# A decoder trunk on one core: S5 parameters and tables, the rows of a shift, and a hold on POOL are moved

## The chip, the core and the metric

The kernel runs on one core of a Trainium2 chip. The metric is the device time of one execution in microseconds; smaller is better. The core has five engines that work side by side and wait for each other through semaphores: TensorE (PE: matmuls, its weight loads are listed as PEld), VectorE (DVE), ScalarE (ACT), GpSimd (POOL) and SyncE (SP, which issues most of the loads). Each engine runs its own instructions strictly in order; an instruction that waits holds up all that stand behind it on its engine.

## What is computed

A trunk of two layers over 512 tokens of width 1024, in float32. Layer 0 mixes the tokens with an S5 state space (32 groups of 16 channels, 64 complex states each) and with HGRN2 (4 heads) side by side, layer 1 with gated linear attention; each mixer is followed by a SwiGLU FFN. In front of each sub-layer stands a norm whose gain and shift come from a conditioning vector c. What matters here is the start of layer 0:

```python
cond = jax.nn.silu(c)
mod = cond @ ada_w[layer] + ada_b[layer]
shift_m, scale_m, gate_m, shift_f, scale_f, gate_f = jnp.split(mod, N_MOD, axis=-1)
h = modulate(rms_norm(x, norm_mix_g[layer]), shift_m, scale_m)
z = h @ ev_w_in[e]
u, hq, hf, hi, hg = jnp.split(z, ...)
# S5: delta = exp(log_step); lam_bar = exp(lam * delta); b_bar = ((lam_bar - 1) / lam) * b
#     states by a linear recurrence over the tokens, y = Re(c . states) + d * u
```

## The kernel before

A float32 product with a weight is made from three matmuls on fp32r halves: high part by high part, low by high, high by low (`proj`, lines 275 to 277). So h is held as `hhi` and `hlo`, and each weight is loaded raw, copied into a high part by ACT (`wsplit`, `whi`) and subtracted into a low part by DVE (`wlo`).

**The gates.** The first norm needs gain (`gsc`) and shift (`mod`) of layer 0. `ada_first` makes them in two halves of 512 columns: half 0 gives the gain and shift of the first four of h's eight tiles, half 1 those of the other four. For each half 16 tiles `ar` of 128x512 are loaded. Eight belong to the scale and are summed up on DVE into `acc` (lines 111 and 116: each instruction adds `ar` times a column of `cond`). Eight belong to the shift. In half 0 all eight are multiplied on PE, as single-row matmuls into `row` (line 405; such a float32 matmul shows as two records). In half 1 (`n` = 4) the first four go to PE and the other four to DVE, into a second sum `acs`. Then small matmuls against ones fold `acc`, `row` (copied to `rsb`) and `acs` into columns (lines 416, 419, 421), and three DVE instructions make `mod` and `gsc`.

**The first products.** x is transposed on PE (`xps`), normalized into `xn` (two blocks by DVE, two by ACT) and transposed again (`xnps`). `norm_out` makes, for each tile of h, `hhi` on ACT, `ht` and `hlo` on DVE. Four projections `u` of S5 (q = 0 to 3) follow: `u_part` does the first four of eight k of one q, the rest is done when the second half of h is there. Behind them come the projections `hq`, `hf`, `hv`, `hg` of HGRN2, head by head, and between these the four blocks of S5.

**S5.** `s5_params` makes the parameters of all groups from `prow` (lambda), `lsrow` (log step) and `drow`: transposes into `pps`, a copy `pc`, then some 70 small DVE instructions (`s5s`, `s5L`), most of 128x16. `s5_tables(q)` makes cosine and sine tables of 128x512 for block q: four products on POOL (`ph` from `s5s` and the index tile `cidx`; `ph` less its rounding; a second product into the `cos` tile; `ph` plus that), on DVE a rounding (`cos<-ph`) and a clamp (`ph<-ph`), on ACT an absolute value and two sines. `s5_in_out` and `s5_mats(q)` make the matrices of block q, mostly on POOL (`s5b`, `bv`, `B`, `W`), copied by ACT into zeroed tiles (`Bd`, `Wd`), transposed on PE (`wnp`) and copied to `wn`. `s5_block` then copies u into `U` (ACT, 16 small pieces), makes `vps` on PE from `wn` and `U`, rotates by the tables, scans on DVE, rotates back, and makes `yp` on PE and `yf` on ACT.

**What sets the order.** The kernel is written as a program; a scheduler puts each engine's instructions in an order from its own estimate of when inputs are there. The code can bend it: `with after(ins):` keeps what is issued inside behind the instruction `ins`, and `tc.high_priority(offset=-3000)` around `s5_params` makes its work yield to all other work. `hold` is a small copy on POOL: with `after(hold)` POOL's work of S5 stands behind it. In the kernel before, one hold waits for the first gate (line 938, for the matrices) and one for the second (line 1001, for the tables). Activation tables are loaded on ACT when a function of another set is next (line 101); exp belongs to one set, silu and sine to another, and `tact` keeps such calls in the order of the code.

Of the kernel before, what the change touches and what calls it, by code (L numbers as in the profile page):

```python
# [8 lines left out]
F32 = mybir.dt.float32  # L9
# [8 lines left out]
P = 128  # L18
# [23 lines left out]
def trunk(  # L42
# [90 lines left out]
    nc.sync.dma_start(out=rows1[112:128, :], in_=norm_ffn_g.rearrange("l (k p) -> (l k) p", p=P))  # L133
    nc.scalar.dma_start(out=rows2[12:16, :], in_=s5_b_glu.rearrange("o (k p) -> (o k) p", p=P))
    nc.scalar.dma_start(out=rows2[16:28, :], in_=hg_lb_logits.rearrange("o (k p) -> (o k) p", p=P))
    nc.scalar.dma_start(out=rows2[28:32, :], in_=od_b_a.rearrange("o (k p) -> (o k) p", p=P))
    nc.scalar.dma_start(out=rows2[8:12, :], in_=s5_d.rearrange("o (k p) -> (o k) p", p=P))

    prow = tt("prow", "s", (16, 4, P))
# [28 lines left out]

    tps = ps_a("tps")
    PE.transpose(tps[:, 0:32], rows2, ident[0:32, 0:32])  # L170
    V.tensor_copy(out=cols2, in_=tps[:, 0:32])
    tact(cond, cols2[:, 0:8], AF.Silu)
    tps = ps_a("tps")
    PE.transpose(tps[:, 0:P], rows1, ident)
    V.tensor_copy(out=cols1, in_=tps[:, 0:P])

# [212 lines left out]

    def ada_first(half, ws, rows=(), n=KT):  # L390


        acc = tt(f"acc01{half}", "sc")
        acs = tt(f"acc00{half}", "X") if n < KT else None
        fp = ps_a(f"row{half}")
        row = fp[0:1, :]
        last = None
        for k in range(KT):
            c_ = cond[:, k : k + 1]
            if k == 0:  # L400
                tsv(V, acc, ws[0], c_, ALU.mult)
            else:
                stt(acc, ws[2 * k], c_, acc, ALU.mult, ALU.add)
            if k < n:
                ins = PE.matmul(row, lhsT=c_, rhs=ws[2 * k + 1], start=(k == 0), stop=(k == n - 1))
            elif k == n:
                tsv(V, acs, ws[2 * k + 1], c_, ALU.mult)
            else:
                stt(acs, ws[2 * k + 1], c_, acs, ALU.mult, ALU.add)
            if k + 1 in rows:  # L410
                last = rows[k + 1](ins)
        rsb = tt(f"rsb{half}", "sc")[0:1, :]
        act(rsb, row, AF.Copy)
        with after(last):
            for m in range(4):
                PE.matmul(fp[:, m : m + 1], lhsT=acc[:, m * P : (m + 1) * P], rhs=ones[:, 0:1], start=True, stop=True)
            for m in range(4):
                o = fp[:, 4 + m : 5 + m]
                ins = PE.matmul(o, lhsT=rsb[:, m * P : (m + 1) * P], rhs=ones[0:1, 0:1], start=True, stop=acs is None)
                if acs is not None:  # L420
                    ins = PE.matmul(o, lhsT=acs[:, m * P : (m + 1) * P], rhs=ones[:, 0:1], start=False, stop=True)
        for i in range(2):
# [145 lines left out]
    def s5_params():  # L568
# [72 lines left out]
        for k in range(2, 5):  # L641
# [6 lines left out]
            ttv(V, L[:, 1, :, k], t0, t1, ALU.add)  # L648
        return L, cr, ci, rho, fh, fl, pc

# [270 lines left out]

    with tc.high_priority(offset=-3000):
        prm = s5_params()
    lb, oml = lbs[0]
    win = ev_w_in[0]
    aw = [ada_first_loads(0)]
# [10 lines left out]
    ada_first(0, aw[0])  # L937
    hold = G.tensor_copy(out=sm("hold", [P, 4]), in_=gsc[:, 0, 0:4])

# [29 lines left out]

    def u_part(q, ks):  # L970
        def run(ins):
            with after(ins):
                return proj(ups[q], wu[q], h, ks=ks)

        return run

    with after(hl):
        fold1 = ada_first(1, aw[1], {4: u_part(0, range(4))}, 4)
    raw.append(wraw(us[3], KT, "u3"))
    with after(hl):  # L980
        wu.append(blocks(wsplit(raw[2], KT, "u2")))
    for q in range(1, 3):
        u_part(q, range(4))(None)
    for m in second:
        norm_out(xns[m - 4], h, 0, 0, 0, m)
    wu.append([])
    for i in range(2):
        w = split(V, raw[3][:, 4 * i : 4 * i + 4, :].rearrange("p k n -> p (k n)"), f"u3{i}", "t", "t")
        wu[3] += blocks([z.rearrange("p (k n) -> p k n", n=P) for z in w])
    u_part(3, range(4))(fold1)  # L990
    tps = ps_b("tps")
    for n in (2, 4):
# [268 lines left out]
```

## Time and profile before

| what | value |
|---|---|
| median of 3 runs | 1348.99 us (1348.24 to 1350.18) |
| the profiled execution | 1345.65 us |
| its span, first to last instruction | 1343.9 us |
| PE busy | 1280.0 us, 95% |
| DVE busy | 766.8 us, 57% |
| ACT busy | 514.1 us, 38% |
| POOL busy | 141.4 us, 11% |
| mean granted clock of PE | 0.974 |

PE is the busy engine overall, but the shares are means over stages that differ: most of PE's idle time lies ahead of 360 us. POOL's work lies mostly between 44 and 280 us. A granted clock of 1.00 is the engine's upper level (2.4 GHz), 0.50 its lower (1.2 GHz). The busy time of an engine counts what an instruction takes from start to end, with the time in it that it is held up by another engine at a shared resource.

### The profile page before, as it was taken

The numbers are of one execution on the slowest core, as the hardware profiler recorded it, in microseconds if no ns is written. First come the engines' busy times: TensorE is split into PE (matmuls) and PEld (weight loads), VectorE is DVE, ScalarE is ACT, GpSimd is POOL, SyncE is SP. The second block draws the span as 40 slices with busy tenths as digits, with TensorE's granted clock in tenths as the row PEclk, the third lists the DMA queues.
The fourth block names the chain that finished last, engine by engine and source line by source line (L and its number), as shares of the span: only waits on it lengthen the run. The fifth ranks groups of instructions, "written<-read, shape, count | busy, mean of one in ns | idle before, by whom it ended". The sixth has DMA issues, their size and how long they took to land.

```text
span 1343.9 us, 18265 instructions
## 1 busy us (share of the span) xinstructions
PE 1280.0 (95%) x6949; PEld 1097.6 (82%) x6949; DVE 766.8 (57%) x1433; ACT 514.1 (38%) x939; POOL 141.4 (11%) x148
## 2 busy tenths in 40 slices
PE   7797999899999999999999999999899999999997
PEld 3577887778888888888888999997888888888886
DVE  5786995787765566566356446657743333333344
ACT  5477358534522222232244433433432222222322
POOL 0593451110100000000010000000100000000000
PEclk9798998999999999999999999999799999999999
DMA  9742531633097669996250322114033323333232
GB/s 305 173 126 79 157 110 38 152 98 102 20 223 189 186 183 230 205 219 185 74 157 21 102 65 78 56 48 133 17 98 103 97 71 99 113 99 104 65 92 79
DMA packets 222824, 159.69 MB, mean 119 GB/s; under 512 B 16752, under 2 KB 195248, under 8 KB 222736
## 3 DMA queue, kind: packets, MB, share of 16 engines
q1 hardware_dynamic: 221696, 157.48, 43.3%
q8 instruction: 54, 0.88, 0.3%
q10 hardware_dynamic: 1040, 1.05, 0.3%
q14 instruction: 34, 0.28, 0.1%
HBM read 156.40 MB, written 2.10 MB: 118 GB/s over the span
## 4 chain that ended last, share of the span: by engine, by line
PE 81%; DVE 10%; ACT 3%; DMA 3%; issue 2%; SPq 0%; POOL 0%; DVEq 0%; ACTq 0%
PE f L275 18%; PE f L276 18%; PE f L277 18%; DMA ar<-in_ada_w_dram 2%; PE op L276 2%; PE lv_g L465 2%; PE op L277 2%; PE op L275 2%; ACT yf L86 1%; PE gr L300 1%; PE gr L301 1%; PE gv L301 1%; PE gr L299 1%; PE gv L300 1%; PE gv L299 1%
## 5 line engine op out<-in xcount | busy, mean ns | idle before, releaser
L276 PE MATMUL f<-hlo_f,whi_f 128*128 128x512 f32 (+1 forms) x736 | 280.8, 383 | 0.4 <-DVE hlo_f L116 0.4
L275 PE MATMUL f<-hhi_f,whi_f 128*128 128x512 f32 (+1 forms) x736 | 279.9, 383 | 0.9 <-ACT hhi_f L86 0.9
L277 PE MATMUL f<-hhi_f,wlo_f 128*128 128x512 f32 (+1 forms) x736 | 280.1, 382 | 0.0
L86 ACT ACTIVATE whi_f<-raw_f 128x1024 fp32r<-128x1024 f32 x88 | 93.3, 1061 | 309.3 <-PE f L276 167.4
L107 DVE TENSOR_TENSOR wlo_f<-raw_f,whi_f 128x1024 fp32r<-128x1024 f32 x88 | 107.7, 1224 | 113.9 <-ACT whi_f L86 113.2
L276 PEld LDWEIGHTS f<-hlo_f,whi_f 128*128 128x128 f32 x736 | 139.2, 189 | 27.2 <-DVE hlo_f L116 1.4
L275 PEld LDWEIGHTS f<-hhi_f,whi_f 128*128 128x128 f32 x736 | 138.9, 190 | 27.5 <-ACT hhi_f L86 1.4
L277 PEld LDWEIGHTS f<-hhi_f,wlo_f 128*128 128x128 f32 x736 | 139.3, 189 | 26.4
L204 DVE SCALAR_TENSOR_TENSOR acc<-ar,cond,acc 128x512 f32<-128x512 f32 x154 | 122.9, 798 | 39.9 <-DMA ar<-in_ada_w_dram 37.8
L277 PE MATMUL f<-hi_g,wlo_c 128*128 128x512 f32 x312 | 121.8, 390 | 0.0
L276 PE MATMUL f<-lo_g,whi_c 128*128 128x512 f32 x312 | 121.7, 390 | 0.0
L275 PE MATMUL f<-hi_g,whi_c 128*128 128x512 f32 x312 | 121.3, 390 | 0.0
L86 ACT ACTIVATE whi_c<-raw_c 128x768 fp32r<-128x768 f32 (+1 forms) x56 | 44.8, 801 | 161.9 <-PE f L276 107.7
L107 DVE TENSOR_TENSOR g<-g,f 128x512 f32<-128x512 f32 x44 | 30.2, 687 | 106.1 <-PE f L277 106.0
L107 DVE TENSOR_TENSOR wlo_c<-raw_c,whi_c 128x768 fp32r<-128x768 f32 (+1 forms) x56 | 50.3, 898 | 60.6 <-ACT whi_c L86 59.1
L275 PEld LDWEIGHTS f<-hi_g,whi_c 128*128 128x128 f32 x312 | 58.6, 188 | 12.1
L276 PEld LDWEIGHTS f<-lo_g,whi_c 128*128 128x128 f32 x312 | 58.6, 188 | 12.1
L277 PEld LDWEIGHTS f<-hi_g,wlo_c 128*128 128x128 f32 x312 | 58.6, 188 | 12.0
L116 DVE SCALAR_TENSOR_TENSOR x<-f,mod,x 128x512 f32<-128x512 f32 (+1 forms) x36 | 24.8, 689 | 40.5 <-PE f L277 40.4
L107 POOL TENSOR_TENSOR na_m<-na_m,nsq_m 128x256 f32<-128x256 f32 x7 | 5.9, 856 | 361.7 <-ACT nsq_m L86 361.7
L300 PE MATMUL gv<-wlo_gv,hhi_m 128*128 128x256 f32 x128 | 36.7, 287 | 0.0
L301 PE MATMUL gv<-whi_gv,hlo_m 128*128 128x256 f32 x128 | 36.6, 287 | 0.0
(668 smaller groups left out, 2651.8 us busy)
## 6 DMA issues: line engine op xcount, KB each, us to landing
raw_f<-in_ffn_w_dram SPq DMA_DIRECT2D x88, 512.0 KB, 4.0
ar<-in_ada_w_dram SPq DMA_DIRECT2D x256, 128.0 KB, 4.2
ar<-in_ada_w_dram SPq DMA_DIRECT2D x64, 256.0 KB, 5.4
raw_c<-in_ffn_w_dram SPq DMA_DIRECT2D x32, 384.0 KB, 3.5
raw_c<-in_ffn_w_dram SPq DMA_DIRECT2D x24, 320.0 KB, 3.2
raw_gv<-in_od_w_in_dram SPq DMA_DIRECT2D x8, 512.0 KB, 3.7
raw_gr<-in_od_w_in_dram SPq DMA_DIRECT2D x8, 512.0 KB, 4.5
raw_o<-in_ev_w_out_dram SPq DMA_DIRECT2D x8, 384.0 KB
```

What stands on the lines that cost most here:

```text
L86: return A.activation(out=o, in_=i, func=f, **kw)
L107: e.tensor_tensor(out=o, in0=a, in1=b, op=op)
L116: V.scalar_tensor_tensor(out=o, in0=a, scalar=s, in1=b, op0=op0, op1=op1)
L204: ins = V.scalar_tensor_tensor(out=acc, in0=w, scalar=c_, in1=acc, op0=ALU.mult, op1=ALU.add)
L275: PE.matmul(ps, lhsT=hi, rhs=ah[:, ts], start=(i == 0), stop=False)
L276: PE.matmul(ps, lhsT=hi, rhs=al[:, ts], start=False, stop=False)
L277: ins = PE.matmul(ps, lhsT=lo, rhs=ah[:, ts], start=False, stop=(i == n - 1))
L299: PE.matmul(o, lhsT=ah[:, s], rhs=hi, start=(k == 0), stop=False)
L300: PE.matmul(o, lhsT=ah[:, s], rhs=lo, start=False, stop=False)
L301: PE.matmul(o, lhsT=al[:, s], rhs=hi, start=False, stop=(k == KT - 1))
L465: PE.matmul(ps[0:nk, w, :].rearrange("p (n b) -> p n b", b=b), lhsT=K[:, w * P : w * P + nk], rhs=qv[:, w * nb : (w + 1) * nb, b:], start= ...
```

## The change

Three things are done. The parameters of S5 lose their low priority, their loads go first on ACT's DMA queue (`cidx` too, the loads of `rows2` behind them), and the tables of all four blocks are made right behind the parameters, with no hold. In the second half (half 1 of `ada_first`) all eight rows of the shift go to PE, `acs` is gone, and the u products of q = 0, 1 are put behind row 4, those of q = 2 behind row 8. The hold of POOL now waits for the last `hlo` of h, for the matrices; the second hold is gone.

```diff
+    cidx = tt("cidx", "X", (P, P))
+    nc.scalar.dma_start(out=cidx, in_=cst[:, P + 2 : 2 * P + 2])
+    nc.scalar.dma_start(out=rows2[12:16, :], in_=s5_b_glu.rearrange("o (k p) -> (o k) p", p=P))
...
-    def ada_first(half, ws, rows=(), n=KT):
+    def ada_first(half, ws, rows=()):
...
-            if k < n:
-                ins = PE.matmul(row, lhsT=c_, rhs=ws[2 * k + 1], start=(k == 0), stop=(k == n - 1))
-            elif k == n:
-                tsv(V, acs, ws[2 * k + 1], c_, ALU.mult)
-            else:
-                stt(acs, ws[2 * k + 1], c_, acs, ALU.mult, ALU.add)
+            with after(last):
+                ins = PE.matmul(row, lhsT=c_, rhs=ws[2 * k + 1], start=(k == 0), stop=(k == KT - 1))
             if k + 1 in rows:
                 last = rows[k + 1](ins)
...
-    with tc.high_priority(offset=-3000):
-        prm = s5_params()
+    tps = ps_a("tps")
+    PE.transpose(tps[:, 0:32], rows2, ident[0:32, 0:32])
+    V.tensor_copy(out=cols2, in_=tps[:, 0:32])
+    prm = s5_params()
+    next(prm)
+    tact(cond, cols2[:, 0:8], AF.Silu)
+    tps = ps_a("tps")
+    PE.transpose(tps[:, 0:P], rows1, ident)
+    V.tensor_copy(out=cols1, in_=tps[:, 0:P])
+    prm = next(prm)
     lb, oml = lbs[0]
+    rot = [s5_tables(q) for q in range(4)]
...
     ada_first(0, aw[0])
-    hold = G.tensor_copy(out=sm("hold", [P, 4]), in_=gsc[:, 0, 0:4])
...
-    with after(hl):
-        fold1 = ada_first(1, aw[1], {4: u_part(0, range(4))}, 4)
-    raw.append(wraw(us[3], KT, "u3"))
     with after(hl):
         wu.append(blocks(wsplit(raw[2], KT, "u2")))
-    for q in range(1, 3):
-        u_part(q, range(4))(None)
...
+    with after(hl):
+        fold1 = ada_first(1, aw[1], {4: u_parts(0, 1), 8: u_parts(2)})
+    raw.append(wraw(us[3], KT, "u3"))
     for m in second:
-        norm_out(xns[m - 4], h, 0, 0, 0, m)
+        hl = norm_out(xns[m - 4], h, 0, 0, 0, m)
...
+    hold = G.tensor_copy(out=sm("hold", [P, 4]), in_=h[KT - 1][1][:, 0:4].bitcast(F32))
     with after(hold):
         bc = s5_in_out(prm, *bcl)
...
-    with after(G.tensor_copy(out=sm("hold", [P, 4]), in_=gsc[:, 0, 4:8])):
-        rot = [s5_tables(q) for q in range(4)]
```

What the scheduler makes of it differs on every engine in the first 300 us; behind that the rows are the same but for a few. Three places matter.

The head of ACT's queue, from the first load to the first squares of x, in the kernel before:

```order
L134 DMA rows_84<-in_s_b_glu_dram 4x128
L135 DMA rows_84<-in_hg_lb_logits_dram 12x128
L136 DMA rows_84<-in_od_b_a_dram 4x128
L137 DMA rows_84<-in_s_d_dram 4x128
L140 DMA prow<-in_s_lam_re_dram 16x128
L141 DMA prow<-in_s_lam_im_dram 16x128
L143 DMA lsrow<-in_s_log_step_dram 16x2
L145 DMA drow<-in_s_d_dram 16x32
L101 ACT_TABLE_LOAD
L86 ACTIVATE cond<-cols_117 128x8
```

and in the changed one:

```order
L135 DMA prow<-in_s_lam_re_dram 16x128
L136 DMA prow<-in_s_lam_im_dram 16x128
L138 DMA lsrow<-in_s_log_step_dram 16x2
L140 DMA drow<-in_s_d_dram 16x32
L142 DMA cidx<-in_cst_dram 128x128
L143 DMA rows_84<-in_s_b_glu_dram 4x128
L144 DMA rows_84<-in_hg_lb_logits_dram 12x128
L145 DMA rows_84<-in_od_b_a_dram 4x128
L146 DMA rows_84<-in_s_d_dram 4x128
L424 DMA mrow<-in_lmask_dram 128x448
L101 ACT_TABLE_LOAD
L86 ACTIVATE lsrow<-lsrow 16x2
```

The loads of S5 stand first, ten loads instead of eight stand ahead of the first table, and that table is now exp's; `cond` has gone behind a second one.

DVE around the first gate, where `mod`, `gsc` and the first `ht` stand (`ht_461` before and `ht_502` after are the same tile of h), in the kernel before:

```order
L107 TENSOR_TENSOR mod<-row_348,cols_116 128x4 x2
L107 TENSOR_TENSOR s5s<-s5s,pc 128x16
L425 SCALAR_TENSOR_TENSOR gsc<-mod,cols_116 128x4
L107 TENSOR_TENSOR s5s<-s5s 128x16 x2
L107 TENSOR_TENSOR s5s<-s5s,pc 128x16 x2
L107 TENSOR_TENSOR s5s<-s5s 128x16 x2
L116 SCALAR_TENSOR_TENSOR ht_461<-xnps_455,gsc,hhi_m_453 128x512
```

and in the changed one:

```order
L107 TENSOR_TENSOR mod<-row_391,cols_118 128x4
L107 TENSOR_TENSOR s5s<-s5L 128x16 x2
L113 TENSOR_SCALAR ph_283<-ph_283 128x512
L411 SCALAR_TENSOR_TENSOR gsc<-mod,cols_118 128x4
L107 TENSOR_TENSOR s5L<-s5s 128x16
L107 TENSOR_TENSOR s5s<-s5L 128x16 x2
L107 TENSOR_TENSOR s5L<-s5s 128x16
L113 TENSOR_SCALAR ph_294<-ph_294 128x512
L107 TENSOR_TENSOR s5s<-s5L 128x16 x2
L107 TENSOR_TENSOR s5L<-s5s 128x16
L116 SCALAR_TENSOR_TENSOR ht_502<-xnps_496,gsc,hhi_m_494 128x512
```

The clamps of the third and fourth table (`ph_283`, `ph_294`) now stand ahead of `gsc` and of the first `ht`; before, all of the tables stood behind the second gate.

POOL from its first products on, in the kernel before:

```order
L938 COPY hold<-gsc 128x4
L107 ISA
L107 TENSOR_TENSOR s5b_650<-bn,s5s 128x256
L107 TENSOR_TENSOR bv_651<-bn,s5s 128x256
L107 TENSOR_TENSOR s5b_655<-bn,s5s 128x256
```

and the last table products and the hold in the changed one:

```order
L107 TENSOR_TENSOR ph_272<-ph_272,cos_273 128x512
L107 TENSOR_TENSOR cos_295<-s5s,cidx 128x512
L107 TENSOR_TENSOR ph_283<-ph_283,cos_284 128x512
L107 TENSOR_TENSOR ph_294<-ph_294,cos_295 128x512
L989 COPY hold<-hlo_m_495 128x4
L107 TENSOR_TENSOR s5b_688<-bn,s5s 128x256
L107 TENSOR_TENSOR bv_689<-bn,s5s 128x256
```

All 16 table products (the last four are shown) stand ahead of the hold, and the hold, which waited for the first `gsc`, waits for an `hlo`.

## Rows read from the trace of the kernel before

**Rows 1.** Stages: us; busy PE, PEld, DVE, ACT, POOL; PEclk, DMA share, GB/s.
```profile
40.00:54.00 14.00, 9.24 (x44) 6.92 (x42) 13.86 (x24) 2.95 (x7) 8.56 (x10) 0.92 0.97 199
54.00:65.00 11.00, 8.95 (x33) 7.61 (x33) 4.07 (x7) 5.28 (x10) 10.77 (x17) 0.50 0.32 71
...
360.00:1344.00 984.00, 967.73 (x5095) 833.58 (x5094) 491.99 (x837) 315.48 (x486) 22.23 (x22) 0.99 0.44 116
```
**Rows 2.** Timeline (start, us, engine, what), PE and DVE around the first gate.
```profile
29.30 1.02 PE L405 MATMUL row<-ar,cond 128*1 128x512 f32 x2
...
31.78 1.05 PE L416 MATMUL row<-ones,acc 128*128 128x1 f32 x8
...
40.27 0.40 PE L276 MATMUL u<-hlo_m,whi_u 128*128 128x512 f32 x1
40.51 0.39 PE L277 MATMUL u<-hhi_m,wlo_u 128*128 128x512 f32 x1
...
35.20 0.75 DVE L116 SCALAR_TENSOR_TENSOR ht<-xnps,gsc,hhi_m 128x512 f32<-128x512 f32 x1
...
38.94 1.67 DVE L362 TENSOR_SCALAR hlo_m<-ht,mod 128x512 fp32r<-128x512 f32 x4
```
**Rows 3.** Timeline, the second gate on PE.
```profile
53.95 1.87 PE L416 MATMUL row<-ones,acc 128*128 128x1 f32 x8 [4.36 <-DVE acc L116]
...
65.11 0.80 PE L276 MATMUL u<-hlo_m,whi_u 128*128 128x512 f32 x1 [2.10 <-DVE hlo_m L362]
...
68.69 0.52 PE L275 MATMUL u<-hhi_m,whi_u 128*128 128x512 f32 x1
```
**Rows 4.** Windows (columns of rows 1), and the roundings of the tables (ns min/median/max).
```profile
25.90:32.70 6.80, 6.80 (x39) 3.70 (x38) 6.70 (x49) 4.49 (x8) 0.00 (x0) 1.00 1.09 362
...
44.88:53.90 9.02, 4.31 (x22) 3.12 (x21) 8.98 (x12) 1.89 (x6) 7.79 (x9) 0.89 1.15 261
70.56:89.30 18.74, 16.60 (x83) 13.66 (x81) 15.46 (x10) 13.33 (x41) 18.74 (x15) 1.00 0.34 107
...
L113 DVE TENSOR_SCALAR cos<-ph x4: 414/832/1503, 67.1 to 75.1; 128x512 f32<-128x512 f32 x4
```
**Rows 5.** Timeline of the start: PE, DVE and ACT.
```profile
10.89 0.48 PE L174 MATMUL tps<-cs,rows 128*128 128x128 f32 x1
...
25.03 0.23 DVE L580 COPY pc<-pps 128x64 f32<-128x64 f32 x1 [0.62 <-PE pps L578]
...
25.25 0.73 DVE L116 SCALAR_TENSOR_TENSOR acc<-ar,cond,acc 128x512 f32<-128x512 f32 x1
...
7.96 0.21 ACT L86 ACTIVATE cond<-cols 128x8 f32<-128x8 f32 x1 [0.70 <-DVE cols L171]
```
**Rows 6.** The tables' instructions by tile (ns min/median/max), and two DVE instructions alone.
```profile
L107 POOL TENSOR_TENSOR ph<-ph,cos x8: 1291/1588/3012, 67.6 to 87.6; 128x512 f32<-128x512 f32 x8
L107 POOL TENSOR_TENSOR ph<-s5s,cidx x4: 1033/1038/1481, 61.1 to 74.0; 128x512 f32<-128x512 f32 x4
...
L107 POOL TENSOR_TENSOR cos<-s5s,cidx x4: 1034/1354/2025, 71.6 to 83.9; 128x512 f32<-128x512 f32 x4
L86 ACT ACTIVATE cos<-ph x4: 615/624/634, 84.5 to 95.5; 128x512 f32<-128x512 f32 x4
...
22.34 1.41 DVE L111 TENSOR_SCALAR xn<-xin,xrs 128x1024 f32<-128x1024 f32 x2
...
30.01 1.22 DVE L107 TENSOR_TENSOR wlo_u<-raw_u,whi_u 128x1024 fp32r<-128x1024 f32 x1
```
**Rows 7.** POOL's matrices, PE's vps of two blocks, and the window from Z to the second.
```profile
48.23 0.62 POOL L107 TENSOR_TENSOR bv<-bn,s5s 128x256 f32<-128x256 f32 x1
...
89.86 2.07 PE L782 MATMUL vps<-U,wn 128*128 128x128 f32 x8 [2.70 <-DVE s5M L107]
...
141.48 0.91 PE vps L782 x8
...
65.10:131.50 66.40, 56.10 (x307) 49.15 (x307) 49.27 (x66) 48.82 (x125) 45.42 (x38) 0.89 0.37 104
```

More of the change, by code (lines that the diff above doesn't have):

```diff
@@ L133, in trunk @@
     nc.sync.dma_start(out=rows1[112:128, :], in_=norm_ffn_g.rearrange("l (k p) -> (l k) p", p=P))
[L134 to L137, printed above, removed]
     prow = tt("prow", "s", (16, 4, P))
@@ L145, in trunk @@
     nc.scalar.dma_start(out=drow, in_=s5_d[0].rearrange("(j c) -> j c", c=32))
+    cidx = tt("cidx", "X", (P, P))
+    nc.scalar.dma_start(out=cidx, in_=cst[:, P + 2 : 2 * P + 2])
+    nc.scalar.dma_start(out=rows2[12:16, :], in_=s5_b_glu.rearrange("o (k p) -> (o k) p", p=P))
+    nc.scalar.dma_start(out=rows2[16:28, :], in_=hg_lb_logits.rearrange("o (k p) -> (o k) p", p=P))
+    nc.scalar.dma_start(out=rows2[28:32, :], in_=od_b_a.rearrange("o (k p) -> (o k) p", p=P))
+    nc.scalar.dma_start(out=rows2[8:12, :], in_=s5_d.rearrange("o (k p) -> (o k) p", p=P))
     ones = const("ones", [P, P])
@@ L167, in trunk @@
     gsc = const("gsc", [P, 4, KT])
[L169 to L175, printed above, removed]
     def ada_loads():
@@ L388, in after @@
         return tc.issue_after(ins.ins) if ins is not None else nullcontext()
-    def ada_first(half, ws, rows=(), n=KT):
+    def ada_first(half, ws, rows=()):
         acc = tt(f"acc01{half}", "sc")
-        acs = tt(f"acc00{half}", "X") if n < KT else None
         fp = ps_a(f"row{half}")
@@ L418, in ada_first @@
                 o = fp[:, 4 + m : 5 + m]
-                ins = PE.matmul(o, lhsT=rsb[:, m * P : (m + 1) * P], rhs=ones[0:1, 0:1], start=True, stop=acs is None)
-                if acs is not None:
-                    ins = PE.matmul(o, lhsT=acs[:, m * P : (m + 1) * P], rhs=ones[:, 0:1], start=False, stop=True)
+                ins = PE.matmul(o, lhsT=rsb[:, m * P : (m + 1) * P], rhs=ones[0:1, 0:1], start=True, stop=True)
         for i in range(2):
@@ L436, in trunk @@
     msk = const("msk", [P, len(LEVELS) * 64], U8)
-    cidx = tt("cidx", "X", (P, P))
-    nc.scalar.dma_start(out=cidx, in_=cst[:, P + 2 : 2 * P + 2])
     mrow = tt("mrow", "X", (P, len(LEVELS) * 64))
@@ L587, in s5_params @@
         lbs.append(lower_bounds())
+        yield
         tsv(V, n, b, 1.0 / (2 * math.pi), ALU.mult, MAGIC, ALU.add)
@@ L648, in s5_params @@
             ttv(V, L[:, 1, :, k], t0, t1, ALU.add)
-        return L, cr, ci, rho, fh, fl, pc
+        yield L, cr, ci, rho, fh, fl, pc
     def s5_in_out_loads():
@@ L968, in trunk, with u_parts @@
     second = range(4, KT)
-    def u_part(q, ks):
+    with after(hl):
+        wu.append(blocks(wsplit(raw[2], KT, "u2")))
+    def u_parts(*qs):
         def run(ins):
-            with after(ins):
-                return proj(ups[q], wu[q], h, ks=ks)
+            for q in qs:
+                with after(ins):
+                    ins = proj(ups[q], wu[q], h, ks=range(4))
+            return ins
         return run
     with after(hl):
-        fold1 = ada_first(1, aw[1], {4: u_part(0, range(4))}, 4)
+        fold1 = ada_first(1, aw[1], {4: u_parts(0, 1), 8: u_parts(2)})
     raw.append(wraw(us[3], KT, "u3"))
-    with after(hl):
-        wu.append(blocks(wsplit(raw[2], KT, "u2")))
-    for q in range(1, 3):
-        u_part(q, range(4))(None)
     for m in second:
-        norm_out(xns[m - 4], h, 0, 0, 0, m)
+        hl = norm_out(xns[m - 4], h, 0, 0, 0, m)
     wu.append([])
@@ L989, in trunk @@
         wu[3] += blocks([z.rearrange("p (k n) -> p k n", n=P) for z in w])
-    u_part(3, range(4))(fold1)
+    u_parts(3)(fold1)
     tps = ps_b("tps")
```

## The prediction

> **What bounds the kernel now.** The table by stage comes first [rows 1]. From 360 us to the end TensorE (PE) is busy for 967.7 of 984 us at a granted clock of 0.99, and no instruction there changes its place among the costly ones. So the change can pay only ahead of that, where PE stands idle or runs below full clock: 4.8 us idle between 40 and 54, a clock of 0.50 from 54 to 65. Whatever the first part hands over earlier or later reaches the end one for one, if the stages in between keep it.
>
> Next come the instructions in order of time. The first half of h waits for the first gate: its first `ht` starts at 35.20, its last `hlo` ends at 40.6 [rows 2]. The second half waits for the second gate: the last sums of `acc` and `acs` on VectorE (DVE) end at 53.9, PE has then waited 4.4 us for them, the small fold matmuls run at half clock (four of them, eight records, take 1.87 us; in the first gate 1.05), and the first low part is there at 65.1 [rows 2, 3]. I call that last moment Z: from then on PE has the second half of the u products, then hq, hf, hv. Z is 65.1 now, and the forecast is where Z goes and what is won or lost behind it.
>
> **The port.** DVE and POOL hinder each other. With POOL at work, 44.88 to 53.90, twelve DVE instructions take 8.98 us; between 70.56 and 89.30, ten take 15.46 us beside fifteen POOL instructions that fill all 18.74 [rows 4]. The four rounds `cos<-ph` are alike and take from 0.41 to 1.50 us, as POOL is there or not [rows 4]. Worked as a sum: the ten DVE instructions alone would be 6.7 us (four clamps and rounds at 0.41, a 0.47, three sums at 0.73, two 1.22), thirteen table products on POOL alone 15.2 (six at 1.03, seven at 1.29), together 21.9 in 18.7 us, a factor of 0.86. The other stretch, counted likewise, has 6.5 and some 5.4 in 9.0, a factor of 0.76. So the two engines' work nearly adds up.
>
> **The change part by part.** *Parameters and tables first.* On ACT's queue the four prow, lsrow and drow loads and cidx now stand ahead of the four rows2 loads, and the table of exp ahead of that of silu, so `cond` comes after the four squares and four copies of x instead of at 7.96 [rows 5]; I put it at about 18. Its users, the sums of the first half, would be late for it only if nothing else held them; on DVE they now stand behind two xn and two rounds as well. The transpose of rows1 is at 10.89 [rows 5]; behind it now stand the copy, the mask cast, the scaling of prow, four transposes and `pc`, some 2.4 us, so pc is there at 13.3 instead of 25.03 [rows 5]. Nineteen small DVE instructions and the chain to `fh` are 2.6 us more (49 instructions, among them two of 1.22 and one of 0.73, filled 6.70 us, which leaves 0.08 for a small one [rows 4], and twice that in a chain). POOL's first table product starts at about 16 (14.5 to 18).
>
> From there the order binds both engines together: DVE's rounds and clamps wait for POOL, POOL's next product for DVE's, and the clamp of the last table, `ph_294`, stands on DVE ahead of the first `ht`. So the first half of h can't start before all 16 POOL products are through. POOL's are 8 at 1.03 and 8 at 1.29, 18.6 us [rows 6]. DVE's from there to the first ht: 55 small ones, 4.5 us; eight rounds and clamps at 0.41, 3.3; two xn at 0.7, 1.4; the eight sums of the first half, 5.6 (0.73 each [rows 5], the first 0.47); two weight splits at 1.22, 2.4: 17.2 us [rows 6]. Together 35.8. At 0.86 that is 31 us, and ht could start at 47. The fold of the first gate needs the last of those sums, which stands 20 DVE rows earlier, and PE will be at half clock by then after long idling, as behind the wait at 53.95 (1.87 for eight [rows 3]); that puts 2 us on it: 49, against 35.2. Ends: 44 at 0.76 without the fold's wait, 54 with no overlap at all. I take 0.86, since that stretch has these very products.
>
> *Rows all on PE, POOL held.* Behind the first half, `acs` (one product, three sums, 2.7 us alone) and its four fold matmuls are gone, POOL is quiet, and DVE needs 1.2 for a split and 5.6 for eight sums. PE needs longer: from ht to the first hlo 3.1 (four at 0.67, one at 0.47); 36 u matmuls at 0.23 (one to the next [rows 2]), 8.3; four rows, each two records and 0.95, 3.8 (1.02 with its end [rows 2]); transposes 0.6; eight folds at full clock 2.1 (four in 1.05 [rows 2], twice); mod and gsc 0.6; hhi, two ht and one hlo 2.5. That is 21.0, and 1.6 for a first stretch at half clock (now eight steps from 65.11 to 68.69, 0.45 each instead of 0.23 [rows 3]): 22.6, where it was 29.9. So Z comes at 71.6 (65 to 77): 6.5 later than now (as early as now to 12 later).
>
> *Behind Z.* Gone from there: POOL's 16 products (61.1 to 89.3), twelve ACT instructions of the tables (0.62 each, 7.5 us [rows 6]) and eight on DVE. New there, since POOL is held until the last hlo is written: s5b, bv, B0, W0 and their memsets, some 25 instructions of about 0.6 us alone [rows 7], 14 us and more beside DVE, and ACT's copies of them. By the order ACT copies B0a after 30 pieces of U, about 20 us behind Z, and wn of block 0 is there at Z + 31; vps of block 0 started at 89.86, Z + 24.8 [rows 7]. So block 0 of S5 comes later by itself, and its yp at about Z + 55, as now. In the meantime PE does other work: in the new order 22 more hf matmuls (0.23) and 45 of hg (0.12) stand ahead of the first vps of block 1, 10.5 us of work, for which there is room, as PE was busy for only 56.1 of the 66.4 us from Z to there, at 0.89 clock [rows 7]. The second vps of block 1 comes at 141.48 now, Z + 76.4 [rows 7]; in the new order only 20 hg matmuls stand ahead of it, not 20 hf and the scores of a head, which gives Z + 70. I take 7 us won behind Z; ends 0 (the S5 chain keeps the pace) and 11 (all of PE's lead stays).
>
> The sum is 6.5 - 7 = -0.5 us. The profiled execution takes 1345.65 us, its span is 1343.9, and the median of the runs is 1348.99, 3.3 above; the difference is put on the median: 1348.5.
>
> **A rule weighed.** The rows show two engines that nearly add up, at 0.76 to 0.86 [rows 4]. The Trainium skill (SBUF — State Buffer, Who interferes with whom) says more: a DVE instruction with two SBUF inputs and a GpSimd one that reads SBUF exclude each other, and the loser waits for the whole instruction. By that rule nothing overlaps, the factor is 1, and the sum would be that of the second rival, not mine; the round that went from 0.41 to 1.50 agrees with it, the factors don't.
>
> **Rivals.** First, POOL's products slip into DVE's gaps (factor 0.76 or less): ht at 44, PE keeps its clock, Z at 65, and with 7 won behind it -7: 1342 (1337 to 1345). For it: DVE has waits for ACT and for the first tiles. Against it: DVE holds some 80 instructions there, nearly all ready.
>
> Second, the slow side: nothing overlaps, ht at 54, Z at 77, and since the same port stretches POOL's B0 and W0 behind the hold, only 3 are won back: +9, 1358 (1353 to 1361). It decides from ht at about 51. For it: 0.41 became 1.50. Against it: 18.7 us held 21.9 of work.
>
> Third, the change makes the tables early but the S5 chain, now started by a later hold, sets the pace behind Z: nothing is won there, +6.5, 1355.5. For it: vps0 comes 6 us later behind Z. Against it: PE, ACT and DVE all have less to do.
>
> Fourth, that it doesn't do what it says: the tables are not made during the first loads. By the sum that is so in every case, since 16 + 18.6 is 34.6 even with DVE silent, where the first half's sums used to end at 26 [rows 5]; it is inside the others.
>
> **How the numbers follow.** 0.2% is 2.7 us, about what a measurement of this kernel can tell from no change. The forecast has 0.44, with its own range of 1344 to 1353: 0.14 of it more than 2.7 us below, 0.23 within, 0.07 above. The first rival has 0.25, the second 0.20, the third 0.11. Faster 0.14 + 0.25 = 0.39, same 0.23, slower 0.07 + 0.20 + 0.11 = 0.38. Cases of both signs hold most of the chance, so the range takes in both outer rivals but for the last of their far ends: 1337 to 1360.
>
> **What will show it.** Right: POOL's products run from about 16 to the middle forties; DVE is full and stretched in that time; the first ht at 47 to 51; the clock drops around 40; no wait of 4 us ahead of the second fold; first low part at 69 to 74; PE less idle between 82 and 143. Wrong: ht before 44 or after 54, or a first vps of block 1 that comes no earlier behind Z while PE stands idle for it.

## The result, and the profile after

| | before | after |
|---|---|---|
| median | 1348.62 us (4 runs, 1347.03 to 1350.18) | 1365.08 us (4 runs, 1359.96 to 1366.59) |
| span of the profiled execution | 1343.9 us | 1362.7 us |
| busy PE / DVE / ACT / POOL | 1280.0 / 766.8 / 514.1 / 141.4 us | 1286.8 / 766.5 / 512.3 / 133.1 us |
| mean granted clock | 0.974 | 0.969 |

The ratio is 1.0115 (95% interval 1.0086 to 1.0145): slower by about 16 us, outside the predicted range of 1337 to 1360. DVE and ACT have as much to do as before. Of the 18.8 us of span, 6.8 are longer busy time of PE, at a lower granted clock, and 12.0 are idle time of PE. The table by stage of the changed kernel (columns as in [rows 1]) shows where PE stands:

```profile
15.90:43.40 27.50, 16.34 (x58) 6.72 (x56) 27.36 (x46) 11.23 (x24) 22.46 (x16) 0.87 1.01 329
44.40:63.10 18.70, 16.71 (x48) 9.91 (x49) 14.33 (x49) 13.31 (x24) 0.00 (x0) 0.59 0.52 121
...
78.20:112.30 34.10, 31.18 (x138) 25.74 (x139) 20.82 (x26) 23.50 (x68) 24.97 (x33) 0.90 0.55 148
112.30:188.80 76.50, 68.79 (x489) 65.32 (x487) 60.33 (x98) 34.65 (x75) 30.95 (x26) 0.92 0.48 129
188.80:273.30 84.50, 67.92 (x450) 59.73 (x448) 55.65 (x105) 57.12 (x139) 17.55 (x16) 0.93 0.25 68
364.60:1362.00 997.40, 980.90 (x5181) 845.51 (x5181) 503.98 (x871) 323.32 (x502) 21.96 (x22) 0.99 0.42 115
```

The first stretch is the tables beside the sums: DVE full, POOL at 22.5 of 27.5 us. In the second PE runs at 0.59 of its clock. The next three go from Z, the moment that the prediction counts from, to the first matmul of S5's GLU: 195.1 us, of which PE is idle for 27.2, and for 16.6 in the last of the three. The same way in the kernel before, to just behind that matmul, has 23.2 us idle in 190.9:

```profile
65.10:256.00 190.90, 167.75 (x1066) 152.40 (x1067) 145.83 (x229) 120.64 (x286) 82.20 (x64) 0.91 0.38 104
```

From 364.6 to the end PE is nearly full again (980.9 of 997.4), as in the last line of [rows 1]: the loss is made ahead of that.

Now the instructions in order of time (start, duration, engine, what, and in brackets the idle time ahead and what ended it). First the two gates of the changed kernel, which answer to [rows 2] and [rows 3]:

```profile
44.48 1.83 PE L404 MATMUL row<-ones,acc 128*128 128x1 f32 x8 [9.28 <-ACT cos L86]
48.03 5.24 PE L397 MATMUL row<-ar,cond 128*1 128x512 f32 x6
50.48 0.75 DVE L116 SCALAR_TENSOR_TENSOR ht<-xnps,gsc,hhi_m 128x512 f32<-128x512 f32 x1
55.82 1.67 DVE L356 TENSOR_SCALAR hlo_m<-ht,mod 128x512 fp32r<-128x512 f32 x4 [2.34 <-PE xnps L953]
72.90 0.95 PE L404 MATMUL row<-ones,acc 128*128 128x1 f32 x8
77.68 0.48 DVE L356 TENSOR_SCALAR hlo_m<-ht,mod 128x512 fp32r<-128x512 f32 x1
78.21 0.79 PE L270 MATMUL u<-hlo_m,whi_u 128*128 128x512 f32 x1 [0.79 <-DVE hlo_m L356]
```

The first `ht` starts at 50.5 instead of 35.2, and Z, the first low part of the second half, comes at 78.2 instead of 65.1. Second, POOL and block 0 of S5, from the hold to its last `yp` matmul, and the GLU's first matmul:

```profile
81.94 0.19 POOL L989 COPY hold<-hlo_m 128x4 f32<-128x4 f32 x1 [38.56 <-DVE hlo_m L356]
94.92 1.19 POOL L107 TENSOR_TENSOR B0b<-B0b 128x256 f32<-128x256 f32 x1
99.56 0.84 ACT L86 ACTIVATE Bd0z<-B0a 64x256 f32<-64x256 f32 x2
110.77 0.60 ACT L86 ACTIVATE wn<-wnp 128x512 f32<-128x512 f32 x1
112.33 1.91 PE L767 MATMUL vps<-U,wn 128*128 128x128 f32 x8
117.92 0.68 DVE L107 TENSOR_TENSOR rz0a<-vps,cos 128x512 f32<-128x512 f32 x1
141.60 0.39 PE L793 MATMUL yp<-rz0b,Wd1z 128*128 128x127 f32 x2
...
273.29 0.79 PE L269 MATMUL glu<-hi_yr,whi_wg 128*128 128x512 f32 x1 [7.75 <-ACT hk L86]
```

POOL waits 38.6 us for the last `hlo`. The matrices come behind it, and the first `vps` starts at 112.3, Z + 34.1, where it was 89.9, Z + 24.8 [rows 7]. The last `yp` matmuls of block 0 start at 141.60. Those of block 0 and of block 3 in the kernel before:

```profile
119.66 0.39 PE L808 MATMUL yp<-rz0b,Wd1z 128*128 128x127 f32 x2
...
242.94 0.39 PE L808 MATMUL yp<-rz3b,Wd1z 128*128 128x127 f32 x2
```

and, in the changed kernel, those of block 3 and what stands on ACT between them and the GLU:

```profile
261.80 0.39 PE L793 MATMUL yp<-rz3b,Wd1z 128*128 128x127 f32 x2
262.23 6.44 ACT L86 ACTIVATE yf<-yp 32x128 f32<-32x128 f32 x16 [8.28 <-PE yp L793]
...
272.64 0.60 ACT L86 ACTIVATE hk<-hf 128x512 f32<-128x512 f32 x1
```

So block 0 is 21.9 us late, block 3 is 18.9 late, and the span is 18.8 longer. The GLU's first matmul waits 7.75 us until ACT has made `hk` of the last head, and `hk` stands on ACT behind `yf` of block 3, which itself waited 8.28 us for `yp`.

### The profile page after: what moved, and what is told of

The parts are those of the page before. It is cut to its first block, busy times and chain, and to the rows that moved or that the text cites. A ratio compares the mean times of both kernels' runs of the same rounds, so it can differ in the third digit from the quotient of the medians.

```text
span 1362.7 us, 18269 instructions
## 1 busy us (share of the span) xinstructions
PE 1286.8 (94%) x6949; PEld 1098.8 (81%) x6949; DVE 766.5 (56%) x1429; ACT 512.3 (38%) x938; POOL 133.1 (10%) x147
## 4 chain that ended last, share of the span: by engine, by line
PE 80%; DVE 9%; ACT 5%; DMA 3%; issue 2%; SPq 1%; DVEq 0%; POOL 0%; ACTq 0%; POOLq 0%
PE f L269 18%; PE f L270 18%; PE f L271 18%; DMA ar<-in_ada_w_dram 2%; ACT yf L86 2%; PE op L270 2%; PE op L269 2%; PE op L271 2%; PE lv_g L449 2%; DVE acc L198 1%; PE gr L294 1%; PE gr L295 1%; PE gr L293 1%; PE gv L295 1%; PE gv L294 1%
## 5 line engine op out<-in xcount | busy, mean ns | idle before, releaser
L269 PEld LDWEIGHTS f<-hhi_f,whi_f 128*128 128x128 f32 x736 | 140.0, 192 | 27.5 <-ACT hhi_f L86 1.4
L116 DVE SCALAR_TENSOR_TENSOR x<-f,mod,x 128x512 f32<-128x512 f32 (+1 forms) x36 | 24.8, 689 | 39.4 <-PE f L271 39.2
```

What stands on the lines that cost most here:

```text
L116: V.scalar_tensor_tensor(out=o, in0=a, scalar=s, in1=b, op0=op0, op1=op1)
L269: PE.matmul(ps, lhsT=hi, rhs=ah[:, ts], start=(i == 0), stop=False)
```

## The experiments

Three theories stood against each other: **T**, that the end follows Z, which the early tables move; **H**, that the late hold of POOL alone is the loss; **R**, that the eight rows on PE at half clock are. After the first four runs H was sharpened to **S**: the end follows block 0 of S5, wherever Z is. The change has three parts that can be taken alone: parameters and tables early (part 1), rows on PE (part 2), the hold (part 3).

All runs in one table. "hlo" is the start of the first `hlo` of the second half, "yp0" and "yp3" the start of the last `yp` row (two matmuls) of blocks 0 and 3, all in us of the profiled execution.

| kernel | ratio to before (95%) | hlo | yp0 | yp3 |
|---|---|---|---|---|
| before | 1 | 63.8 | 119.7 | 242.9 |
| after | 1.0115 (1.0086 to 1.0145) | 77.7 | 141.6 | 261.8 |
| no_hold | 0.9990 (0.9976 to 1.0004) | 77.7 | 123.6 | 238.7 |
| tables_only | 1.0036 (1.0022 to 1.0049) | 78.2 | 123.2 | 243.8 |
| rows_only | 1.0028 (1.0014 to 1.0043) | 60.5 | 125.1 | 251.1 |
| no_tables | 1.0046 (1.0027 to 1.0065) | 57.2 | 129.6 | 252.2 |
| hold_only | 1.0069 (1.0054 to 1.0084) | 58.7 | 132.1 | 252.2 |
| hold_gain2 | 1.0129 (1.0114 to 1.0144) | 75.4 | 136.6 | 262.4 |
| params_rows | 1.0025 (1.0014 to 1.0036) | 63.8 | 122.5 | 245.7 |
| one_table_gate | 0.9943 (0.9928 to 0.9957) | 64.5 | 114.7 | 231.2 |
| chain_delay | 1.0110 (1.0080 to 1.0140) | 63.6 | 142.6 | 261.3 |
| one_table | 1.0074 (1.0054 to 1.0094) | 61.2 | 135.9 | 252.7 |
| one_table_split | 0.9993 (0.9974 to 1.0011) | 69.1 | 117.2 | 241.5 |
| tables_later | 0.9963 (0.9945 to 0.9981) | 66.2 | 109.3 | 234.5 |

Over the 14 kernels the ratio's correlation with hlo is 0.13 (with the last of the four `hlo` 0.14), with yp0 0.95, with yp3 0.98. From yp0 to yp3 it takes 115 to 126 us in every one of them.

What ends that stage is not the same in all. In eight kernels (before, after, rows_only, no_tables, hold_only, hold_gain2, chain_delay, one_table) the GLU's first matmul waits 2.7 to 10.0 us for a copy of the last head (`hk` on ACT or `hq` on DVE), which comes behind `yf` of block 3, and it starts 10 to 13 us after yp3. In the other six it waits for nothing and follows PE's own matmuls, 13 to 24 us after yp3, as in one_table_gate:

```profile
250.36 0.28 PE L298 MATMUL hg<-whi_hg,hlo_m 128*128 128x256 f32 x1
250.48 0.41 PE L272 MATMUL glu<-hi_yr,whi_wg 128*128 128x512 f32 x1
```

So a late S5 chain sets the start of the GLU, but an early one leaves it to PE, and a lead need not be worth what a delay costs.

**no_hold: the changed kernel without its late hold.**

```diff
     ada_first(0, aw[0])
+    hold = G.tensor_copy(out=sm("hold", [P, 4]), in_=gsc[:, 0, 0:4])
...
-    hold = G.tensor_copy(out=sm("hold", [P, 4]), in_=h[KT - 1][1][:, 0:4].bitcast(F32))
```

> The changed kernel, but POOL's hold waits for the first gain again, as in the kernel before; the early tables and the rows on PE stay. Theory T (the tables, made ahead of the first gate, move Z from 65 to 78, and S5's chain keeps that): first ht at 50, Z at 77 to 81, first vps of block 0 at 90 to 98 instead of 112, time 1353 to 1358. Rival H (the late hold alone is the loss): Z may stay late, but the time comes back to 1349 give or take 3. Rival R (the rows on PE at half clock are the loss): nothing changes against the changed kernel, 1362 to 1367.

Measured: 1345.86 us. In its timeline the gates are as late as in the changed kernel, POOL starts the matrices at 49.6 instead of 82.1, and block 0 waits only for u and its copy U:

```profile
49.48 0.19 POOL L935 COPY hold<-gsc 128x4 f32<-128x4 f32 x1 [5.87 <-DVE gsc L414]
77.65 0.84 DVE L359 TENSOR_SCALAR hlo_m<-ht,mod 128x512 fp32r<-128x512 f32 x1
83.41 0.57 ACT L86 ACTIVATE wn<-wnp 128x512 f32<-128x512 f32 x1
87.44 2.80 ACT L86 ACTIVATE U<-u 32x128 f32<-32x128 f32 x10
93.18 1.95 PE L770 MATMUL vps<-U,wn 128*128 128x128 f32 x16
123.58 0.39 PE L796 MATMUL yp<-rz0b,Wd1z 128*128 128x127 f32 x2
```

The second half is 14 us late and nothing of it reaches the end: T and R fall; H holds, with a time 0.1 us below its range. With this one instruction where it stood before, nothing of the loss is left.

**tables_only, rows_only, no_tables: the parts apart.** tables_only is the kernel before with part 1; rows_only with part 2; no_tables with parts 2 and 3. Their diffs are the pieces of the diff above, for part 1:

```diff
-    with tc.high_priority(offset=-3000):
-        prm = s5_params()
+    prm = s5_params()
...
+    rot = [s5_tables(q) for q in range(4)]
...
-    with after(G.tensor_copy(out=sm("hold", [P, 4]), in_=gsc[:, 0, 4:8])):
-        rot = [s5_tables(q) for q in range(4)]
```

> The kernel before with only the first part of the change: parameters and all four tables made during the first loads; rows of half 1 split between PE and DVE, and the hold on the first gain, as before. T: first ht at 49 to 52, Z at 77 to 82, time 1354 to 1362. H and R both: 1349 give or take 3, since their suspects are as before.

> The kernel before with only the second part: all eight rows of half 1 on PE, no second sum on DVE; tables and holds as before. T: first ht at 35 as before, Z at 60 to 65, time 1343 to 1349. R: the eight rows at half clock take PE 8 us and more, Z no earlier than 67, time 1352 to 1358. H: 1349 give or take 3.

> The changed kernel with the first part undone: rows on PE and the hold on the last hlo stay, parameters late and the tables behind the second gain, as before. T: first ht at 35, Z at 58 to 64, and even with the first vps of block 0 some 34 us behind Z the time is 1343 to 1350. H: first vps of block 0 at Z + 34 or later, as POOL now has matrices and tables both behind Z, time 1355 to 1362.

Measured: 1351.39, 1351.48 and 1354.04 us. tables_only is below T's range although its first `ht` is at 52.3 and its hlo at 78.2. In rows_only hlo comes 3.3 us earlier and in no_tables 6.6 us earlier than before, and both are slower, so T misses both; R asked rows_only for Z at 67 or later and 1352 to 1358; its first `hlo` is there at 60.5, and the time is 0.5 us below. But only that first one is early: the fourth comes at 71.6, 4.2 us later than before, so what tells against R is no_hold, which has the rows on PE at no loss. H's ranges hold the first two and miss the third by 1 us, but H gives the first two no cost, and each has one, of 0.36% and 0.28%; so H alone is not all. Nor do the parts add up: part 1 costs 0.36%, parts 2 and 3 0.46%, all three 1.15%. With no_hold beside rows_only, the tables without the hold win 0.4%; with the changed kernel beside no_tables they lose 0.7% with it. So, with the rows on PE, the hold is what makes the early tables dear: it ties POOL's matrices to the second half, which the tables delay. Why they cost 0.36% in tables_only, without a late hold, no run shows.

**hold_only: the hold alone.**

```diff
-    hold = G.tensor_copy(out=sm("hold", [P, 4]), in_=gsc[:, 0, 0:4])
...
-        norm_out(xns[m - 4], h, 0, 0, 0, m)
+        hl = norm_out(xns[m - 4], h, 0, 0, 0, m)
...
+    hold = G.tensor_copy(out=sm("hold", [P, 4]), in_=h[KT - 1][1][:, 0:4].bitcast(F32))
```

> The kernel before with only the third part: POOL's hold for the matrices waits for the last hlo; all else as before. Theory S (what the end follows is the first vps of block 0 of S5, not Z): POOL is quiet until about 61, so Z comes at 62 to 65, but the matrices then stand among the tables on POOL and the first vps of block 0 moves from 90 to 97 to 101; time 1351 to 1357. Rival T (the end follows Z): 1344 to 1349.

Measured: 1357.06 us. From its timeline:

```profile
58.65 0.48 DVE L362 TENSOR_SCALAR hlo_m<-ht,mod 128x512 fp32r<-128x512 f32 x1
62.91 0.19 POOL L994 COPY hold<-hlo_m 128x4 f32<-128x4 f32 x1 [60.69 <-DVE hlo_m L362]
100.58 1.92 PE L782 MATMUL vps<-U,wn 128*128 128x128 f32 x8
132.09 0.39 PE L808 MATMUL yp<-rz0b,Wd1z 128*128 128x127 f32 x2
```

With POOL quiet the second half comes 5 us earlier than before, block 0 10.7 us later at its first `vps`, and the kernel loses 9.4 us. The two moments move in opposite directions, and the time goes with block 0. S has the direction and the first `vps`; its time is missed by 0.1 us (1357 at most), and Z, at 59.2, is earlier than its 62 to 65.

**chain_delay: a delay put into block 0.** The kernel before, with copies on POOL in the middle of block 0's rotation:

```diff
         ttv(G, t[2], t[2], t[3], ALU.subtract)
+        for k in range(4 if q == 0 else 0):
+            G.tensor_copy(out=t[3], in_=t[2])
+            G.tensor_copy(out=t[2], in_=t[3])
```

> The kernel before with one thing added: eight copies of 128x512 on POOL in the chain of block 0 (rz0c to rz0d and back, four times), between two instructions of its rotation; the results are the same. A copy should take about 1 us on POOL, so yp of block 0 ends some 8 us later (at 126 to 130 instead of 119.8), and nothing ahead of 100 us moves, so Z stays at 65. Theory S (the end follows S5's block 0): 1352 to 1358. Rival T (the end follows Z, PE has other work in the meantime): 1347 to 1350.

Measured: 1362.82 us. From its timeline, one of the copies and what became of the chain:

```profile
63.61 1.26 DVE L362 TENSOR_SCALAR hlo_m<-ht,mod 128x512 fp32r<-128x512 f32 x1
89.67 2.08 PE L782 MATMUL vps<-U,wn 128*128 128x128 f32 x8 [2.77 <-DVE s5M L107]
107.32 0.95 POOL L793 COPY rz0c<-rz0d 128x512 f32<-128x512 f32 x1
128.40 1.54 DVE L204 SCALAR_TENSOR_TENSOR acc<-ar,cond,acc 128x512 f32<-128x512 f32 x2 [4.61 <-DMA ar<-in_ada_w_dram]
131.59 1.36 DVE L797 TENSOR_TENSOR_SCAN rz0d<-s5s,rz0c 128x128 f32<-128x128 f32 x4
142.64 0.39 PE L811 MATMUL yp<-rz0b,Wd1z 128*128 128x127 f32 x2
```

Nothing ahead of 100 us has moved: Z and the first `vps` are where they were. Five of the eight copies take 0.95 us, about as expected, but the chain loses 23.0 us and not 8, since its second scan now stands on DVE behind weight splits and sums that wait for loads (4.6 us in the row shown). So S's time is missed too, by 4.8 us, and T's by 12.8. With the delay that came the price fits: yp0 is as late as in the changed kernel (142.6 and 141.6), and so is the end (ratios 1.0110 and 1.0115). The loss of the change is made here again without its tables, its rows or its hold. It is not block 0 alone that is late, though: the splits of `wlo_hg` and a head's `hq` stand on DVE behind the same waiting sums.

**hold_gain2: a smaller dose of the hold.**

```diff
-    hold = G.tensor_copy(out=sm("hold", [P, 4]), in_=h[KT - 1][1][:, 0:4].bitcast(F32))
+    hold = G.tensor_copy(out=sm("hold", [P, 4]), in_=gsc[:, 0, 4:8])
```

> The changed kernel with POOL's hold on the second gain (75.2 in its trace) instead of the last hlo (81.9); the rest as changed. A dose between no_hold (first vps of block 0 at 93, 1345.9) and the changed kernel (112, 1365.1). S: first vps of block 0 at 103 to 109, Z as late as in the changed kernel, time 1355 to 1362, about 1 us for 1 us of vps. T: 1363 to 1367, as Z does not move.

Measured: 1365.15 us, so S's time fails, and T's range (1363 to 1367) has it, though block 0 is earlier than in the changed kernel by 5.7 us at its first `vps` (106.65) and by 5.0 at yp0. The lead is still there in block 2, whose last `yp` matmul starts at 214.3 instead of 222.1. In the timeline of this kernel it is lost in block 3, between PE's transposes and ACT's copy of them:

```profile
223.35 0.60 PE L730 MATMUL wnp<-cs,Bd1z 128*128 128x128 f32 x4
...
227.75 1.28 ACT L101 ACT_TABLE_LOAD   x1
229.05 1.67 ACT L86 ACTIVATE yf<-yf 128x512 f32<-128x512 f32 x3
...
233.84 0.57 ACT L86 ACTIVATE wn<-wnp 128x512 f32<-128x512 f32 x1
```

The transposes are done at 224, the copy `wn` comes at 233.8, behind `yf`, weight copies and the gates of a head on ACT; yp3 is at 262.4, as in the changed kernel, where the copy came about 3 us behind its transposes. T's hit doesn't rest on Z, which came 2.3 us earlier here at no gain; but S as it stood, 1 us for 1 us of block 0, is refuted for leads. A lead at block 0 can be given back by what a later order puts ahead of block 3.

**params_rows and one_table_gate: what block 0 needs beside its matrices.** params_rows is the kernel before with the parameters early and the rows on PE, tables and holds as before. one_table_gate is the changed kernel with one of four tables early and the hold on the first gain:

```diff
-    rot = [s5_tables(q) for q in range(4)]
+    rot = [s5_tables(0)]
...
     ada_first(0, aw[0])
+    hold = G.tensor_copy(out=sm("hold", [P, 4]), in_=gsc[:, 0, 0:4])
...
-    hold = G.tensor_copy(out=sm("hold", [P, 4]), in_=h[KT - 1][1][:, 0:4].bitcast(F32))
...
+    with after(G.tensor_copy(out=sm("hold", [P, 4]), in_=gsc[:, 0, 4:8])):
+        rot += [s5_tables(q) for q in range(1, 4)]
```

> The kernel before with S5's parameters early and the rows on PE, the tables behind the second gain and the matrices behind the first, as before: POOL's matrices no longer wait for parameters, only for the load of b (about 44). S: Z at 60 to 64, wn of block 0 ready well ahead of u, first vps of block 0 at Z + 15 as in no_hold, so 76 to 84, unless the tables hold the first rotation until 88 to 95; time 1338 to 1347. T: 1343 to 1346, by Z alone. If the port makes DVE late for the second gate: Z as before and 1347 to 1351.

> The changed kernel with only the first of four tables early, the other three behind the second gain, and the hold on the first gain. The price of four early tables is 15 us of the first ht (35.2 to 50.5); for one table I expect a quarter of POOL's products, first ht at 38 to 42. S: Z at 63 to 70, first vps of block 0 at 80 to 88, time 1338 to 1347. T: Z a little later or as before, 1347 to 1352.

Measured: 1351.27 and 1340.62 us. In both the first `vps` starts at 79.1. In params_rows it is of no use; its timeline:

```profile
98.59 0.84 DVE L113 TENSOR_SCALAR ph<-ph 128x512 f32<-128x512 f32 x1
99.35 0.68 DVE L107 TENSOR_TENSOR rz0a<-vps,cos 128x512 f32<-128x512 f32 x1
```

The rotation `rz0a` stands on DVE behind the clamps of all four tables, as in the kernel before, and starts later than there (96.98), so yp0 doesn't gain. S's time, which went by `vps`, is missed, and T's too; the third case that was named, Z as before and 1347 to 1351, is missed by 0.3 us. With one table early the rotation starts at 89.45:

```profile
38.46 2.76 DVE L116 SCALAR_TENSOR_TENSOR ht<-xnps,gsc,hhi_m 128x512 f32<-128x512 f32 x4 [0.47 <-ACT hhi_m L86]
79.14 1.95 PE L770 MATMUL vps<-U,wn 128*128 128x128 f32 x16
89.45 0.68 DVE L107 TENSOR_TENSOR rz0a<-vps,cos 128x512 f32<-128x512 f32 x1
114.68 0.39 PE L796 MATMUL yp<-rz0b,Wd1z 128*128 128x127 f32 x2
```

Parameters and one table cost the first `ht` 3.3 us (the parameters alone 3.9, in params_rows), with four tables it is 15.3. yp0 is 5.0 us earlier than before, yp3 11.7, and this kernel beats both, by 0.57% (0.43 to 0.72) against the kernel before. S's time holds, T's (1347 to 1352) doesn't.

**one_table, one_table_split, tables_later: one part of that kernel at a time.** one_table has the hold of the changed kernel, one_table_split the rows as before (the `ada_first` and `u_part` of the kernel before), and tables_later makes the other tables behind block 0's rotation:

```diff
         ttv(G, z[1], z[1], cosT, ALU.mult)
+        if q == 0:
+            with after(G.tensor_copy(out=sm("hold", [P, 4]), in_=z[1][:, 0, 0:4])):
+                rots.extend(s5_tables(i) for i in range(1, 4))
```

> The kernel of the label one_table_gate (1340.6) with POOL's hold on the last hlo, as the change has it; the hold is the only difference. S: Z a few us earlier (60 to 64, POOL is quiet), block 0's matrices late, its first vps at 97 to 101 instead of 79, time 1350 to 1357, so the hold costs 10 to 16 us here. T: 1336 to 1341.

> The kernel of the label one_table_gate (1340.6) with the rows of half 1 split between PE and DVE again: the rows are the only difference. S: Z may come up to 4 us later, but block 0 waits for its rotation on DVE and not for PE; time 1339 to 1346. T: as much later as Z, 1343 to 1348.

> The kernel of the label one_table_gate (1340.6) with the other three tables behind block 0's rotation on POOL instead of behind the second gain. S: DVE is less hindered between 65 and 90, block 0's rotation starts at 82 to 86 instead of 89.5, its yp ends at 107 to 112 instead of 114.7, and the time is 1334 to 1340, unless the table of block 1 comes too late for its first rotation (then 1341 to 1348). T: Z at 65 as before, no gain, 1339 to 1342.

Measured: 1358.18, 1347.31 and 1342.67 us. In one_table hlo is 3.3 us earlier and yp0 21.2 later, and it costs 17.6 us: the hold's price again. T, with 1336 to 1341, falls again; S is missed by 1.2 us in time, and its first `vps` (97 to 101) comes at 104.4. one_table_split doesn't tell S and T apart: its time is inside T's range and 1.3 us above S's, but hlo comes only 4.6 us later, yp0 2.5, and yp3 10.3, so 2.1 of its 6.7 us are lost behind the one moment or 4.2 behind the other; rows on PE are worth about 0.5% in that kernel, where they cost 0.3% in rows_only. tables_later does what was expected of it up to yp0 (109.3, rotation at 84.2) and is no faster for it: S's 1334 to 1340 is missed. The time lies in the range that S gave for a late table of block 1, but blocks 1 and 2 keep the lead (7.2 and 6.8 us at their last `yp` matmuls, against one_table_gate). It is lost in block 3, whose yp3 is 3.2 us later, and PE's last `hg`, which the GLU follows directly, starts at 257.1 instead of 250.4.

## Why the prediction was wrong

**The step that failed is the premise.** "Whatever the first part hands over earlier or later reaches the end one for one, if the stages in between keep it", with Z as that moment, and then "7 won" behind it from a count of what stands ahead on PE. In the terms of the sum, Z came 13.1 us later instead of 6.5, and 5.7 were lost behind it where 7 were to be won. Z is not the moment that counts: no_hold has it 14 us late at no loss, hold_only 5 us early at a loss of 9. What counts here is the S5 chain, late from block 0 on. Its `yp` followed Z by 51 to 55 us in the kernel before, and I put it at "about Z + 55, as now"; the last came at Z + 63.4. The second `vps` of block 1, predicted for Z + 70 instead of Z + 76, came at 161.07, Z + 82.9. The first, named as a sign of being wrong, came at Z + 78.6 instead of Z + 66.4. PE did get the earlier work that I counted (54.8 us busy of 82 to 143 instead of 50.7), but it is no bound there: its last `hg` product of the heads starts at 252.8, as in the kernel before (252.7), though Z is 13.1 us later, and then PE stands idle at the end of the chain. What was read as room for PE was the chain's pace.

**The third rival had the mechanism.** "The S5 chain, now started by a later hold, sets the pace" stood there with a chance of 0.11 and a price of 6.5 us, by Z alone. The argument against it, that PE, ACT and DVE all have less to do, says nothing about a chain whose links wait for each other. Its price was too small twice: Z itself came later, and block 0 another 8.8 behind it. The second rival's Z of 77 nearly came, but not by its way: it wanted the first `ht` at 54, which came at 50.5, and 3 us won behind Z.

**Z at 78.2 instead of 71.6.** The port term held. pc was there at 12.70 (13.3 predicted), POOL's first product at 15.86 (16), `cond` at 18.66 (18), the first `ht` at 50.5 (49, range 44 to 54). In the 27.5 us from 15.9 to 43.4 lie 18.6 us of POOL's products and 13 to 15 of DVE's (seven sums, two xn, five rounds and clamps, two splits at their times alone, 29 small ones at 0.08 to 0.16), which makes a factor of 0.81 to 0.87. (The low end that the prediction gave for `ht`, 44, is 43.2 by its own terms, 16 and 0.76 of 35.8. And the round of 0.42 us at 69.03 in the kernel before ran beside a POOL product that took 3.01: there POOL's product was the one stretched, so "as POOL is there or not" is too simple.) The mis-sized term is the 22.6 from ht to Z, which took 27.7. I charged 2 and 1.6 us to a first stretch at half clock; the stretch from 44.4 to 63.1 was granted 0.59, which on 16.71 busy us of PE is 6.9, by estimate. PE had waited 9.3 us ahead of it, and in it stood three rows of half 1 (six records, 5.24 us), ahead of the first u. Beside that all four `hlo` waited 2.3 us for transposes on PE, which waited for ACT's copies `xnT` behind the sines of the early tables.

**The rest.** The hold's own cost was seen: `wn` of block 0 was predicted for Z + 31 and came at Z + 32.6, behind 30 pieces of U on ACT, and the 4.4 us wait ahead of the second fold is gone, as said. The mistake was to call this harmless. The order of the changed kernel showed it: POOL's matrices behind the last `hlo`, and all of block 0 behind them.

**The sum as it should have been.** Block 0's `yp` 13.1 us later by Z and 8.8 later behind it, 21.9; the blocks behind give back about 3 (120.2 us instead of 123.3): 18.9 at yp3, 18.8 in the span.

## What to carry to other kernels

Before a change ahead of a stage is costed, find out which chain sets the end of that stage: mark the last instruction that PE waits for at its end, follow it back block by block, and cost the change at the first link of that chain, not at the last instruction of the stage before. A hold that keeps a slow engine quiet ties everything behind it to the moment that it waits for; a delay that was harmless before becomes the delay of the whole chain. Make early only what the first link needs: with the hold on the first gain, one table early won 0.57%, and four won nothing clear of noise (0.10%); four with the late hold lost 1.15%. And once the chain is early, look again at what ends the stage: here PE's own matmuls did, and a further lead of block 0 (tables_later) won nothing.

## What the runs showed of the hardware

Small DVE instructions can cost far more beside POOL than their size says. The first two of these rows are alike in size and kind on DVE, in the changed kernel. The first started as POOL went from one product to the next (at 20.15); the third row is the POOL product that runs at 22.91:

```profile
20.13 0.15 DVE L107 TENSOR_TENSOR lbm<-lbm 128x4 f32<-128x4 f32 x1
22.91 1.23 DVE L107 TENSOR_TENSOR lbm<-lbm 128x4 f32<-128x4 f32 x1
22.41 1.71 POOL L107 TENSOR_TENSOR ph<-ph,cos 128x512 f32<-128x512 f32 x1 [1.22 <-DVE cos L113]
```

The second ends at 24.14, with POOL's product (24.12). Here a small instruction paid for what was left of a POOL product; the sum had it at 0.08. The Trainium skill (SBUF — State Buffer, Who interferes with whom) says that of a DVE instruction with two SBUF inputs, as this `lbm<-lbm` has, and a GpSimd one that reads SBUF, the one that comes later waits until the other is through. This row agrees, while the factor of 0.81 to 0.87 over the whole stretch shows that part of the two engines' work did overlap. The prediction called the round that went from 0.41 to 1.50 us to witness for that rule, but a round has one SBUF input, so the rule as quoted doesn't speak of it. Instructions with one input were held up all the same: a 128x16 `s5s<-s5s` (TENSOR_SCALAR) at 27.39 took 1.23 us and ended with a POOL product, at 28.6.

What sets the 38 to 42 us that a block of S5 takes on average (115 to 126 for three) stays open. PE's waits in the chain name ACT's copies `yf` and `wn` and the rotation on DVE in turn, and the runs changed the order of all of them at once.
